# The planner of the first mixer and the second block charges a change between parts of TensorE's array, and runs one part in longer spells

## The chip, the cores and the metric

The kernel runs on one core of one Trainium2 chip, as one launch. The metric is the device time of the launch in microseconds (us), the median of three runs. Five engines work side by side, each in the order of its own program: PE (TensorE, matrix products; PEld is its weight loading), DVE (VectorE), ACT (ScalarE), POOL (GpSimd) and SP, which here only starts transfers. They wait for one another through semaphores.

## The reference, cut to what matters

All arrays are float32, one sequence of 256 tokens, width 1024. The first block is a modulated mixer (a state-space part, an attention part and a convolution part) followed by a mixture of 32 experts; the second block is an RWKV layer with 16 heads of 64, then a differential attention layer, each followed by a gated embedding. The part that this change moves most is the RWKV layer:

```python
    rkvg = jnp.einsum('cbsd,cde->cbse', xmix[:4], w_in)
    ...
    def step(state, inp):
        r_t, w_t, k_t, v_t, kk_t, a_t = inp
        s_kk = jnp.einsum('bhij,bhj->bhi', state, kk_t)
        state = (state * w_t[:, :, None, :]
                 - s_kk[..., None] * (kk_t * a_t)[:, :, None, :]
                 + v_t[..., None] * k_t[:, :, None, :])
        return state, jnp.einsum('bhij,bhj->bhi', state, r_t)
    ...
    _, y = lax.scan(step, state0, (seq_first(r), seq_first(decay), seq_first(k),
                                   seq_first(v), seq_first(kk), seq_first(a)))
    ...
    return y @ w_out
```

## The kernel before, in words

**Stages.** `mixer` does the first block up to the routing (until about 230 us in the profile), `moe` the experts (until about 688 us), `second` the rest. Within `second`, the RWKV layer runs until about 1051 us, then come its output projection, the eight pairs of attention heads (`diff_head`, about 1110 to 1230 us) and the last projection.

**The RWKV layer.** The recurrence is cut into four chunks of 64 tokens and done as products. Two of the 16 heads form one unit n, of eight. `dense` (a long list of matmuls written `pd<-xm,whl`, 768 of them, 256 columns each, 128 rows by 128 columns of the array) makes r, k, v and the gate: each product of two float32 numbers is three matmuls in type float32r of split parts. Each unit n then goes through three pieces of code, each a chain of small steps: `rwkv_inner` (scales, decays, the matrices BK, AR and PQ; matmuls into pm and pq), `rwkv_invert` (a triangular inverse in five levels: 8 matmuls `pi<-T,PQ` of 64 by 64, a copy by ACT, 8 matmuls `pi<-Gt,T`, a masked copy and a transpose by DVE, then the next level) and `rwkv_chunks` (four chunks in a row: `pe<-VU,PQ`, a copy by DVE, `pe<-W,Gt`, a copy by DVE, `pe<-VU,KB`, and so on). At most two units may be in the same piece. These small matmuls are float32 and use a part of the array: 64 by 64, 64 by 128, 128 by 64 or 32 by 32. The 768 dense matmuls use the whole. A float32 matmul shows as two records in the trace, a float32r one as one.

**What sets the order.** In `mixer` and `second` (not in `moe`) no order is written by hand. Every piece is a generator (a stream) that yields its next operations. `Plan` keeps, for each engine, the time at which it will be free by the planner's own costs (`cost`, L198), and for each tile the times of its last uses. `Mux.run` (L317) picks again and again: of all operations that head a stream it takes the engine of the one that can start first, adds that engine's hold to this time, and issues, of the operations of that engine that can start by then, the one of best rank. Ranks are small for the chains (0 to 2) and 3 for `dense`, so a small matmul that is ready goes ahead of a dense one. `start` (L194) gives the time at which an operation can start: when its inputs are ready and the engine free. `clocked` (L231) adds up how much work PE gets and doubles a matmul's cost when it was little; `cool` (L242) says that PE has had little work lately (below `HEAT`), and then `run` lets only float32r matmuls through, if one is ready. `enter` (L248) books the operation. What the streams issue is always the same set of instructions; the planner decides their order on each engine, and that order is fixed in the program. All recorded operations carry line 72.

Of the kernel before, what the change touches and what calls it, by code (L numbers as in the profile page):

```python
# [44 lines left out]
NR = _o  # L45


HEAT = 3500, 3550
HOLD = 250
WAIT = (60, 105, 110, 150), (60, 120, 120, 150)  # L50
FIRST = 3
# [85 lines left out]
class Plan:  # L137
# [8 lines left out]
    def __init__(s, nc):  # L146
        s.nc = nc
        s.at = {}
        s.use = {}
        s.free = {}  # L150
        s.work, s.past, s.part, s.heat = {}, [], False, HEAT[0]
        s.log = []
        s.cur = None
        for n in ("tensor", "vector", "scalar", "gpsimd", "sync"):
            setattr(s, n, Lane(s, getattr(nc, n), n))

    def reset(s):

        s.at = {"dma": 0.0, "scalar": 10e3, "gpsimd": 11e3, "tensor": 16e3, "vector": 15.8e3}
        s.use, s.free, s.work, s.past, s.heat = {}, {}, {}, [], HEAT[1]  # L160

    def __getattr__(s, x):
        return getattr(s.nc, x)
# [29 lines left out]

    def start(s, op, lag=0):  # L194
        eng = op.lane.name
        return op.ready if eng == "sync" else max(op.ready + lag * (eng == "tensor"), s.at.get(eng, 0.0))

    def cost(s, op):  # L198
        eng, name, out, ins = op.lane.name, op.op, op.outs[0], op.ins
        n = 1  # L200
        for _, c in (ins[-1] if name in ("tensor_reduce", "bn_stats") else out).ap[1:]:
            n *= c
        if eng == "tensor":
            if name == "transpose":
                return 109
            if ins[0].dtype == F32R:
                return max(107, n / 2.4) + 2
            m = out.ap[0][1]
            if m > 64:
                return max(214, n * 4 / 2.4 + 4)  # L210
            if s.box(out)[0]:
                return 22 if m <= 32 else 53
            return max(107, n * 4 / 2.4) + 2
        psum = any(x.space == PSUM for x in (out, *ins))
        if eng == "vector":
            fast = name in ("tensor_scalar", "tensor_copy", "memset") and not psum
            return 68 + n * (0.52 if fast else 1.04) + 61 * s.pointers(op)
        if eng == "scalar":
            return (51 if psum else 93) + n * 0.835 + 93 * s.pointers(op)
        if eng == "sync":  # L220
            return n * 512 / 355.0
        return 150 + n * 2.1

    @staticmethod
    def pointers(op):
# [2 lines left out]
            x += [op.a[i] if len(op.a) > i else None for i in ((2,) if op.op[0] == "s" else (2, 3))]  # L228
        return sum(isinstance(v, bass.AP) for v in x)

    def clocked(s, start, dur, op):  # L231

        w = int(start / 3413.3)
        n = 1 if op.ins[0].dtype == F32R else 2
        for _, c in op.outs[0].ap[1:]:
            n *= c
        n *= op.ins[0].ap[0][1] / 128 * (dur > 53)
        s.work[w] = s.work.get(w, 0.0) + n
        s.past.append((start, n))
        return dur if s.work.get(w - 1, 0.0) > 3060 else 2 * dur  # L240

    def cool(s, t):  # L242

        while s.past and s.past[0][0] < t - 3413.3:
            s.past.pop(0)
        return sum(n for _, n in s.past) < s.heat

    def enter(s, op, r):  # L248
# [6 lines left out]
        else:  # L255
            start = s.start(op)
            if eng == "tensor":

                part = op.outs[0].ap[0][1] <= 64
                dur = s.clocked(start, dur + 54 * (s.part and op.ins[0].dtype == F32R), op)  # L260
                s.part = part
            end = start + dur
            s.at[eng] = end
            if op.op == "dma_start":
# [19 lines left out]
class Mux:  # L284
# [32 lines left out]
    def run(s):  # L317
        pl = s.plan
        while s.st:
# [7 lines left out]
                            x.then()  # L327
            if not s.st:
                break
            can = [(pl.start(o, x.lag), x.rank if o.lane.name == "tensor" else x.side, i, x, o) for i, x in enumerate(s.st) for o in x.head]  # L330
            assert can, [(x.gen.__name__, x.gen.gi_frame.f_lineno) for x in s.st]
            t, _, _, x, o = min(can, key=lambda c: c[:3])
            eng = o.lane.name
# [2368 lines left out]
```

## Time and profile before

| what | value |
| --- | --- |
| median of 3 runs | 1298.44 us (1293.02 to 1301.1) |
| the profiled execution | 1295.23 us, of which the span from first to last instruction is 1293.3 us |
| busy over the span | PE 92%, PEld 63%, DVE 51%, ACT 34%, POOL 10% |
| mean granted TensorE clock | 0.948 of 2.4 GHz |

The page cuts the span into 40 slices; each digit is the busy share of an engine in tenths, and PEclk is the granted clock in tenths of full speed. TensorE has two clock levels, 2.4 GHz (1.00 in the rows) and 1.2 GHz (0.50); a value between them is a mean over a stretch. PE counts as busy from the start of a matmul to its modelled end, and matmuls overlap, so a PE that is always busy may still issue more or fewer of them in the same time. How fast it issues is read from the distance of two starts in the timeline.

### The profile page before, as it was taken

What the parts mean: (1) busy time and instruction counts of PE and PEld (TensorE: products, weight loads), DVE (VectorE), ACT (ScalarE), POOL (GpSimd) and SP (SyncE); (2) the same over time, 40 slices, a digit from 0 to 9 for tenths busy, and PEclk for the clock granted to TensorE, in tenths of its full rate; (3) what the DMA queues carried; (4) which work ended last, traced back from release to release, by engine and by line L of the source; (5) the groups of instructions that cost most, each with busy time, mean ns of one, the idle gap of its engine ahead of it and who ended that gap; (6) DMA issues with size and microseconds to landing.
All of it is one profiled execution on the core that took longest, in us unless ns stands there. A gap on an engine that the chain in (4) does not pass through costs nothing. (4 is left out here: it accounts for less than half of the span.)

```text
span 1293.3 us, 20461 instructions
## 1 busy us (share of the span) xinstructions
PE 1185.9 (92%) x7906; PEld 809.4 (63%) x7906; DVE 660.4 (51%) x1782; ACT 435.3 (34%) x1074; POOL 127.6 (10%) x358
## 2 busy tenths in 40 slices
PE   5999987999999989898986989999999989899896
PEld 3777886344343444444356867877777656888775
DVE  5695766111111111111027952576676677788885
ACT  3564543011110101111024721333344445655543
POOL 1000000000000000000000211222222002022212
PEclk8999996999999999999996975899999999899999
DMA  9658566899999999999983421111212342544422
GB/s 374 276 225 331 217 254 259 335 421 421 420 420 421 420 420 421 420 421 420 420 324 101 143 70 38 38 54 39 70 57 92 129 141 86 170 157 148 141 82 75
DMA packets 52628, 306.14 MB, mean 237 GB/s; under 512 B 5680, under 2 KB 10288, under 8 KB 25392
## 3 DMA queue, kind: packets, MB, share of 16 engines
q1 hardware_dynamic: 52368, 304.67, 60.1%
q8 instruction: 64, 1.05, 0.3%
q14 instruction: 36, 0.29, 0.1%
q0 software_dynamic: 160, 0.13, 0.1%
HBM read 302.55 MB, written 2.10 MB: 236 GB/s over the span
## 5 line engine op out<-in xcount | busy, mean ns | idle before, releaser
L366 PE MATMUL pgu<-w,xe 128*64 128x512 f32 x1024 | 233.0, 595 | 15.6 <-DMA w<-moe 15.6
L366 PEld LDWEIGHTS pgu<-w,xe 128*64 128x64 f32 x1024 | 80.9, 137 | 155.8 <-issue 116.6
L72 PE MATMUL pd<-xm,whl 128*128 128x256 f32 x768 | 149.3, 324 | 5.5 <-ACT xm L72 3.9
L72 DVE TENSOR_TENSOR whl<-raw,whl 128x512 fp32r<-128x512 f32 x192 | 128.4, 683 | 11.0 <-ACT whl L72 10.3
L72 ACT CAST whl<-raw 128x512 fp32r<-128x512 f32 x192 | 111.3, 618 | 40.5 <-PE pd L72 23.7
L72 PEld LDWEIGHTS pd<-xm,whl 128*128 128x128 f32 x768 | 112.9, 207 | 18.5 <-ACT xm L72 4.5
L366 PE MATMUL py<-w,hT 128*64 128x512 f32 (+1 forms) x528 | 116.6, 583 | 7.0 <-ACT hT L1408 7.0
L1433 DVE SCALAR_TENSOR_TENSOR yl<-py,ws,yh 128x512 fp32r<-128x512 f32 (+1 forms) x33 | 24.2, 734 | 123.4 <-ACT yh L1432 123.4
L366 PEld LDWEIGHTS py<-w,hT 128*64 128x64 f32 x528 | 40.7, 137 | 71.4 <-issue 54.7
L1352 POOL TENSOR_TENSOR PW<-P,wt 128x256 f32<-128x256 f32 x16 | 9.9, 617 | 617.7 <-PE pw L1413 213.4
L1432 ACT ACTIVATE yh<-py,ws 128x512 fp32r<-128x512 f32 (+1 forms) x33 | 22.2, 675 | 119.6 <-PE acc L366 66.1
L1398 DVE TENSOR_TENSOR hid<-hid,pgu 128x512 f32<-128x512 f32 x16 | 11.0, 688 | 98.2 <-PE pgu L366 98.1
L1397 DVE SCALAR_TENSOR_TENSOR hid<-hid,pgu 128x512 f32<-128x512 f32 x16 | 11.0, 688 | 96.8 <-ACT hid L1396 96.7
L72 PE MATMUL pd<-hh,whl 128*128 128x256 f32 x384 | 59.0, 295 | 1.4 <-ACT whl L72 0.8
L72 PE MATMUL pd<-xx,whl 128*128 128x256 f32 x384 | 54.2, 287 | 1.7 <-ACT whl L72 0.9
L72 PEld LDWEIGHTS pd<-hh,whl 128*128 128x128 f32 x384 | 50.6, 194 | 4.8 <-issue 2.6
L72 PE MATMUL pd<-whl,hh 128*128 128x512 f32 x192 | 52.4, 407 | 1.1 <-ACT hh L72 1.1
L72 PEld LDWEIGHTS pd<-xx,whl 128*128 128x128 f32 x384 | 48.9, 192 | 3.5 <-ACT whl L72 1.2
L72 PE MATMUL a<-hl,wh 128*128 128x256 f32 x160 | 47.1, 294 | 1.5 <-DVE hl L72 1.5
L72 PE MATMUL a<-hh,wh 128*128 128x256 f32 x160 | 46.8, 292 | 0.6 <-DVE x L72 0.6
L72 PE MATMUL a<-hh,wl 128*128 128x256 f32 x160 | 46.5, 291 | 0.0
L72 DVE TENSOR_TENSOR wl<-w,wh 128x512 fp32r<-128x512 f32 (+1 forms) x60 | 39.3, 692 | 10.5 <-ACT wh L72 10.4
(506 smaller groups left out, 2230.3 us busy)
## 6 DMA issues: line engine op xcount, KB each, us to landing
w<-moe SPq DMA_DIRECT2D x190, 1024.0 KB, 19.8
w<-ada SPq DMA_DIRECT2D x12, 2048.0 KB, 11.8
raw<-awin SPq DMA_DIRECT2D x32, 512.0 KB, 3.4
raw<-bwin SPq DMA_DIRECT2D x32, 512.0 KB, 3.5
w<-win SPq DMA_DIRECT2D x5, 2048.0 KB, 12.0
raw<-pleg SPq DMA_DIRECT2D x16, 512.0 KB, 3.3
w<-wout SPq DMA_DIRECT2D x2, 2048.0 KB, 8.6
raw<-awout SPq DMA_DIRECT2D x8, 512.0 KB, 3.4
```

Of the source, the lines that this page charges most:

```text
L72: r = s.fn(*s.a, **s.k)
L366: return s.nc.tensor.matmul(out, lhsT=lhsT, rhs=rhs, start=first, stop=last, **kw)
L1352: G.tensor_tensor(PW.rearrange(four, e=2), P[:, :, o:o + 128].bitcast(F32).rearrange(four, e=2), wt[:, :, 2 * i:2 * i + 2, None].to_broadc ...
L1397: V.scalar_tensor_tensor(hid, hid, 1.0, pgu[0], op0=OP.add, op1=OP.mult)
L1398: V.tensor_tensor(hid, hid, pgu[1], op=OP.mult)
L1432: A.activation(y[0], p, AF.Copy, scale=ws)
L1433: V.scalar_tensor_tensor(y[1], p, ws, y[0].bitcast(F32), op0=OP.mult, op1=OP.subtract)
```

## The change

The planner's model of PE is replaced; no operation is added or taken away. The part of the array that a matmul uses (`form`: rows and columns, each 128, 64 or 32) is now looked at. `start` adds 95 ns (138 when the clock is thought low) to the start of a matmul whose part differs from the one before it (`change`). `run` picks by a new time `come`: the same with that surcharge, but without it once PE has stayed long enough in its present kind of work (400 ns in float32, 1400 ns in float32r). The costs of small matmuls are set anew, a float32r one costs 9 ns more, the first float32r matmul behind another part 105 ns more, and the work by which the planner guesses the clock is weighted by part and kind. `HEAT` goes from 3500 and 3550 to 3300.

```diff
-HEAT = 3500, 3550
 ...
+WORK = {(128, 128): 3.2, (64, 64): 1.7, (64, 128): 2.2, (128, 64): 1.9, (32, 32): 1.5, (128, 32): 1.0}
+HEAT = 3300, 3300
+LONG = 400, 1400
 ...
     def start(s, op, lag=0):
         eng = op.lane.name
-        return op.ready if eng == "sync" else max(op.ready + lag * (eng == "tensor"), s.at.get(eng, 0.0))
+        if eng == "tensor":
+            return max(op.ready + lag, s.at.get(eng, 0.0) + s.change(op))
+        return op.ready if eng == "sync" else max(op.ready, s.at.get(eng, 0.0))
+
+    def come(s, op, lag=0):
+
+        t = s.start(op, lag)
+        if op.lane.name == "tensor":
+            at = s.at.get("tensor", 0.0)
+            if at - s.since > (LONG[s.whole]):
+                t = max(op.ready + lag, at)
+        return t
 ...
             if ins[0].dtype == F32R:
-                return max(107, n / 2.4) + 2
-            m = out.ap[0][1]
-            if m > 64:
-                return max(214, n * 4 / 2.4 + 4)
-            if s.box(out)[0]:
-                return 22 if m <= 32 else 53
-            return max(107, n * 4 / 2.4) + 2
+                return max(107, n / 2.4) + 11
+            k, m = s.form(op)
+            if k == m:
+                if k == 128:
+                    return max(214, n * 4 / 2.4 + 4)
+                return 58 if m == 64 else 31
+            if k == 64:
+                return max(107, n * 4 / 2.4) * (0.75 if n > 128 else 1) + 2
+            if m == 64:
+                return 58 if n < 8 else 165 if n <= 64 else 109
+            return 13 if s.box(out)[0] else max(107, n * 2 / 2.4) + 14
 ...
+    def form(op):
+
+        if op.op == "transpose":
+            return 128, 128
+        return tuple(128 if n > 64 else 64 if n > 32 else 32 for n in (op.ins[0].ap[0][1], op.outs[0].ap[0][1]))
 ...
+    def change(s, op):
+
+        op = getattr(op, "ops", [op])[0]
+        if s.part is None or s.part == s.form(op) or (s.part, s.form(op)) == ((64, 128), (128, 128)):
+            return 0
+        return 138 if s.cold(s.at.get("tensor", 0.0)) else 95
 ...
     def clocked(s, start, dur, op):
 ...
+        part, whole = s.form(op), op.ins[0].dtype == F32R
+        cold = s.cold(start)
+        if cold:
+            dur = 2 * (dur - 11) if whole else 1.9 * dur
+
+        if whole and part != s.part:
+            dur += 165 if cold else 105
+        n = 1.0 if whole else 1.5 if op.op == "transpose" else WORK[part]
 ...
-            can = [(pl.start(o, x.lag), x.rank if o.lane.name == "tensor" else x.side, i, x, o) for i, x in enumerate(s.st) for o in x.head]
+            can = [(pl.come(o, x.lag), x.rank if o.lane.name == "tensor" else x.side, i, x, o) for i, x in enumerate(s.st) for o in x.head]
```

**How the order moves.** Counted over PE's whole program of `second` (3244 matmuls in both), two neighbours use different parts of the array 540 times before and 331 times after; from matmul 200 to matmul 2000, the RWKV layer with its chains, 506 times and 299 times. In `mixer` it is 57 times in both, in `moe` 68 times in both.

The first place is on PE, in the inverse of the first unit, where `dense` (pd, the whole array) fills in between the 64 by 64 matmuls of a level (pi; `x8` stands for eight matmuls). A row is the source line, the operation, the tile written from the tiles read, and the size of the output. Before, in the trace at about 765 to 768 us:

```order
L72 MATMUL pi_5804<-T,PQ 64x64 x7
L72 MATMUL pq<-AR,BK 128x128
L72 MATMUL pd_5713<-xm_4945,whl 128x256 x3
L72 MATMUL pi_5804<-Gt,T 64x64 x5
L72 MATMUL pd_5713<-xm_4945,whl 128x256
L72 MATMUL pi_5804<-Gt,T 64x64
L72 MATMUL pd_5713<-xm_4945,whl 128x256
L72 MATMUL pi_5804<-Gt,T 64x64
L72 MATMUL pd_5713<-xm_4945,whl 128x256
L72 MATMUL pi_5804<-Gt,T 64x64
L72 MATMUL pd_5713<-xm_4945,whl 128x256
```

The same levels of the first unit's inverse in the changed program:

```order
L76 MATMUL pi_5817<-T,PQ 64x64 x8
L76 MATMUL pm<-ident,rkv 128x128 x2
L76 MATMUL pd_5748<-xm_4945,whl 128x256 x8
L76 MATMUL pm<-ident,BK 128x128 x4
L76 MATMUL pi_5817<-Gt,T 64x64 x8
L76 MATMUL pi_5858<-T,PQ 64x64 x8
L76 MATMUL pd_5748<-xm_4945,whl 128x256 x3
L76 MATMUL pm<-la,whl 128x256
```

The eight matmuls of a level, which stood in four pieces with single dense matmuls between them, now stand together, and so do the dense ones.

The second place is on PE in the middle of the layer, the third level of the fourth unit's inverse, beside the chunks of the third unit (pe). Before:

```order
L72 MATMUL pi_6947<-T,PQ 64x64 x3
L72 MATMUL pd_6889<-xm_4945,whl 128x256 x2
L72 MATMUL pe_6915<-VU,KB 128x128
L72 MATMUL pe_6915<-VU,PQ 64x64
L72 MATMUL pd_6889<-xm_4945,whl 128x256
L72 MATMUL pe_6915<-VU,PQ 64x64
L72 MATMUL pd_6889<-xm_4945,whl 128x256
L72 MATMUL pi_6947<-T,PQ 64x64
L72 MATMUL pd_6889<-xm_4945,whl 128x256 x2
L72 MATMUL pi_6947<-T,PQ 64x64 x3
```

The same level of the same unit in the changed program:

```order
L76 MATMUL pe_6968<-W,Gt 64x64 x2
L76 MATMUL pi_6979<-T,PQ 64x64 x8
L76 MATMUL pm<-ident,rsq_y 64x128
L76 MATMUL pe_6968<-VU,KB 128x128
L76 MATMUL pe_6968<-VU,PQ 64x64 x2
L76 MATMUL pi_6979<-Gt,T 64x64 x8
L76 MATMUL pm<-ident,rsq_y 64x128
L76 MATMUL pe_7024<-ST_4959,AR 128x128
L76 MATMUL pe_7024<-VU,PQ 64x64 x2
```

The dense matmuls are gone from between the pieces of the two chains; they stand further on, eleven in a row.

The third place is SP's list of the weight loads in the mixer (`win` for the dense products there, `ada` for the modulation). Before:

```order
L72 DMA w<-ada 128x4096 x3
L72 DMA w<-win 128x4096
L72 DMA w<-ada 128x4096
L72 DMA w<-win 128x4096
L72 DMA w<-ada 128x4096 x2
```

And in the changed program:

```order
L76 DMA w<-ada 128x4096 x2
L76 DMA w<-win 128x4096
L76 DMA w<-ada 128x4096 x3
L76 DMA w<-win 128x4096
L76 DMA w<-ada 128x4096
```

The first of these `win` loads stands one place earlier on the queue, the second behind one `ada` load more.

## Rows read from the trace of the kernel before

**Rows 1.** The page: span, busy time and share, busy tenths by slice, clock.
```profile
span 1293.3 us, 20461 instructions
PE 1185.9 (92%) x7906; PEld 809.4 (63%) x7906; DVE 660.4 (51%) x1782; ACT 435.3 (34%) x1074; POOL 127.6 (10%) x358
PE   5999987999999989898986989999999989899896
PEclk8999996999999999999996975899999999899999
```

**Rows 2.** Busy time by stage: the stretch, its length, busy us (instructions), clock, DMA.
```profile
core 0: us, PE busy (x) PEld busy (x) DVE busy (x) ACT busy (x) POOL busy (x), PEclk, DMA share, GB/s
60.00:160.00 100.00, 100.00 (x747) 80.24 (x745) 74.51 (x226) 57.30 (x147) 0.00 (x0) 1.00 0.66 263
...
240.00:660.00 420.00, 396.60 (x1990) 177.69 (x1987) 68.82 (x113) 46.48 (x74) 9.25 (x15) 1.00 1.01 420
...
688.00:740.00 52.00, 45.80 (x324) 43.05 (x325) 47.78 (x120) 30.34 (x76) 5.55 (x10) 0.87 0.44 141
740.00:756.00 16.00, 9.75 (x81) 7.82 (x80) 12.69 (x32) 4.80 (x12) 7.37 (x23) 0.90 0.41 133
756.00:771.00 15.00, 15.00 (x109) 11.63 (x110) 4.95 (x12) 3.66 (x10) 0.00 (x0) 0.73 0.15 45
771.00:821.00 50.00, 50.00 (x295) 37.24 (x294) 15.89 (x43) 9.67 (x26) 3.38 (x13) 0.50 0.11 35
821.00:1024.00 203.00, 198.77 (x2083) 155.40 (x2083) 141.84 (x417) 79.52 (x207) 51.21 (x192) 1.00 0.22 73
...
1120.00:1220.00 100.00, 92.25 (x740) 85.28 (x738) 86.43 (x206) 56.42 (x168) 23.21 (x78) 1.00 0.46 149
```

**Rows 3.** Waits of PE from 756 to 1024 us: total us, times, longest.
```profile
PE pe L72 <- DVE yn L72: 1.7, 2, 1.4
PE pi L72 <- DVE T L72: 0.9, 2, 0.5
```

**Rows 4.** Timeline of PE at full clock: start, length, operation, records.
```profile
766.04 0.33 PE L72 MATMUL pi<-Gt,T 64*64 64x64 f32 x2
766.30 0.38 PE L72 MATMUL pd<-xm,whl 128*128 128x256 f32 x1
766.61 0.33 PE L72 MATMUL pi<-Gt,T 64*64 64x64 f32 x2
```

**Rows 5.** Timeline of PE, the same pattern at half clock.
```profile
773.16 0.47 PE L72 MATMUL pi<-Gt,T 64*64 64x64 f32 x2
773.56 0.58 PE L72 MATMUL pd<-xm,whl 128*128 128x256 f32 x1
774.07 0.47 PE L72 MATMUL pi<-Gt,T 64*64 64x64 f32 x2
```

**Rows 6.** Timeline of PE, longer runs of one part at full clock.
```profile
714.01 12.10 PE L72 MATMUL pd<-xm,whl 128*128 128x256 f32 x98
...
827.93 1.09 PE L72 MATMUL pd<-xm,whl 128*128 128x256 f32 x7
828.95 0.45 PE L72 MATMUL pi<-Gt,T 64*64 64x64 f32 x8
829.33 0.49 PE L72 MATMUL pq<-AR,BK 64*128 64x128 f32 x2
...
864.03 0.68 PE L72 MATMUL pi<-Gt,T 64*64 64x64 f32 x16
864.64 0.44 PE L72 MATMUL pm<-ident,rkv 128*128 128x128 f32 x2
```

**Rows 7.** Waits of PE from 735 to 756 us.
```profile
PE pq L72 <- DVE BK L72: 3.6, 2, 3.0
PE pm L72 <- POOL rsq_y L72: 2.7, 1, 2.7
```

**Rows 8.** Waits of PE in the first 60 us.
```profile
PE x L72 <- DMA w<-ada: 4.2, 2, 3.5
```

**Rows 9.** DMA issues on the page: tile, queue, count, KB each, median us to landing.
```profile
w<-win SPq DMA_DIRECT2D x5, 2048.0 KB, 12.0
```

More of the change, by code (lines that the diff above doesn't have):

```diff
@@ L45 @@
 NR = _o
-HEAT = 3500, 3550
+SPELL = 3413.3
+WORK = {(128, 128): 3.2, (64, 64): 1.7, (64, 128): 2.2, (128, 64): 1.9, (32, 32): 1.5, (128, 32): 1.0}
+HEAT = 3300, 3300
+LONG = 400, 1400
 HOLD = 250
@@ L150, in __init__ @@
         s.free = {}
-        s.work, s.past, s.part, s.heat = {}, [], False, HEAT[0]
+        s.work, s.past, s.part, s.heat, s.whole, s.since = {}, [], None, HEAT[0], False, 0.0
         s.log = []
@@ L159, in reset @@
         s.at = {"dma": 0.0, "scalar": 10e3, "gpsimd": 11e3, "tensor": 16e3, "vector": 15.8e3}
-        s.use, s.free, s.work, s.past, s.heat = {}, {}, {}, [], HEAT[1]
+        s.use, s.free, s.work, s.past, s.part, s.heat, s.whole, s.since = {}, {}, {}, [], None, HEAT[1], False, 0.0
     def __getattr__(s, x):
@@ L229, in pointers, with cold @@
         return sum(isinstance(v, bass.AP) for v in x)
-    def clocked(s, start, dur, op):
-        w = int(start / 3413.3)
-        n = 1 if op.ins[0].dtype == F32R else 2
+    @staticmethod
+    def form(op):
+        if op.op == "transpose":
+            return 128, 128
+        return tuple(128 if n > 64 else 64 if n > 32 else 32 for n in (op.ins[0].ap[0][1], op.outs[0].ap[0][1]))
+    def cold(s, t):
+        return s.work.get(int(t / SPELL) - 1, 0.0) < 2880
+    def change(s, op):
[3 more added lines that the diff above has]
+        return 138 if s.cold(s.at.get("tensor", 0.0)) else 95
+    def clocked(s, start, dur, op):
+        part, whole = s.form(op), op.ins[0].dtype == F32R
[5 more added lines that the diff above has]
+        n = 1.0 if whole else 1.5 if op.op == "transpose" else WORK[part]
         for _, c in op.outs[0].ap[1:]:
             n *= c
-        n *= op.ins[0].ap[0][1] / 128 * (dur > 53)
-        s.work[w] = s.work.get(w, 0.0) + n
+        w, end = int(start / SPELL), start + dur
+        behind = max(0.0, min(1.0, (end - (w + 1) * SPELL) / dur))
+        s.work[w] = s.work.get(w, 0.0) + n * (1 - behind)
+        s.work[w + 1] = s.work.get(w + 1, 0.0) + n * behind
         s.past.append((start, n))
-        return dur if s.work.get(w - 1, 0.0) > 3060 else 2 * dur
+        if whole != s.whole:
+            s.whole, s.since = whole, start
+        s.part = part
+        return dur
     def cool(s, t):
-        while s.past and s.past[0][0] < t - 3413.3:
+        while s.past and s.past[0][0] < t - SPELL:
             s.past.pop(0)
@@ L257, in enter @@
             if eng == "tensor":
-                part = op.outs[0].ap[0][1] <= 64
-                dur = s.clocked(start, dur + 54 * (s.part and op.ins[0].dtype == F32R), op)
-                s.part = part
+                dur = s.clocked(start, dur, op)
             end = start + dur
```

## The prediction

> **What bounds the kernel now.** I read the page first, then the busy time by stage, then PE's waits and its timeline in the one stage that the change reorders much. The page says that PE is busy for 92% of the span and that its clock has a hole in the slices around 60% of the span [rows 1]. By stage [rows 2], the experts (240 to 660 us) are bound by transfers: 420 GB/s at a DMA share of 1.01, and the planner doesn't order that stage. In the mixer PE is busy in all of 60 to 160 us. From 688 to 740 us DVE is busy for 47.78 of 52 us: it prepares the mixed inputs of the RWKV layer, and PE waits for it. From 756 to 1024 us, the body of the RWKV layer, it is the other way round: PE is busy for 15.00 of 15, 50.00 of 50 and 198.77 of 203 us, DVE for 70% of the last stretch, and PE's waits in the 268 us are a few us [rows 3]. So whatever PE issues faster there comes off the end, until DVE or the chains of small steps are late.
>
> Two things make PE slow in that body. The first is the change between parts of the array. At full clock one dense matmul and one 64 by 64 matmul (two records) that alternate take 766.61 - 766.04 = 0.57 us a pair [rows 4]. In a long run a dense matmul takes 12.10 / 98 = 0.123 us; a run of 16 records of 64 by 64 takes 864.64 - 864.03 = 0.61 us, one of 2 records 766.30 - 766.04 = 0.26 us, so a record costs (0.61 - 0.26) / 14 = 0.025 us [rows 4, 6]. The pair's own work is 0.123 + 0.05 = 0.17 us; the other 0.40 us goes to its two changes, 0.20 us each. A second reading gives a little less: seven dense matmuls and a run of 8 records take 829.33 - 827.93 = 1.40 us, of which 0.86 + 0.20 us is work, which leaves 0.34 us for two changes, 0.17 us each [rows 6]. The second thing is the clock: 0.50 in all of 771 to 821 us, 0.73 in the 15 us ahead of it, 1.00 from 821 us on [rows 2]. Ahead of the fall to 0.50 PE did such pairs [rows 4], and it was still in them 2 us after [rows 5]. There a pair takes 774.07 - 773.16 = 0.91 us [rows 5], 1.6 times as long, so a us at the low clock does 0.63 us of work and loses 0.37 us.
>
> **The change part by part.** Nothing is added or removed; the order of `second` and of `mixer` moves.
>
> *Fewer changes of part.* 540 - 331 = 209 fewer in `second`, nearly all in the RWKV layer (506 to 299), where PE is the bound. At 0.17 to 0.20 us they are worth 36 to 42 us at full clock; I take 40, near the upper price, because most of the removed ones lie between dense and small matmuls, as in the first place shown.
>
> *The clock.* The 50 us at the low clock lose 50 x 0.37 = 19 us. What stood ahead of the fall, pairs with one dense matmul each, is replaced there by runs of eight dense ones and of eight or sixteen small ones, so PE does more work in the same time; I take the 19 us in full, with 0 as the other bound. The earlier dip, in the 0.73 of 756 to 771 us, I leave as it is: it follows PE's waits for DVE and POOL at 740 to 756 us (9.75 of 16 us busy [rows 2, 7]), which the change doesn't remove.
>
> The Trainium skill, "TensorE: Matmul & The Clock Gate", the section on what is happening, puts it so that the throttle is the state of an idle engine and that activity releases it. The rows don't bear that out as it stands: PE has no idle time in those 50 us and yet has the low clock. By that rule alone the fall would come of the waits before it, nothing in the order would lift it, and the 19 us would stay; that is the second case below.
>
> *What is late next.* Without these 59 us the body takes 268 - 59 = 209 us, and DVE still needs 4.95 + 15.89 + 141.84 = 162.7 us in it [rows 2]: 78% of the time instead of 61%. How much PE then waits I read from two stretches: at DVE 70% (821 to 1024 us) PE was idle for 2%, at DVE 86% (1120 to 1220 us) for 7.75% [rows 2]. On the line between them 78% gives 5%, 10 us of 209, against 4 us now: 6 us more. A chain's small matmul that is ready now also waits behind longer dense runs: eleven, as in the second place shown, are 11 x 0.123 = 1.4 us. Most of that is hidden, because three pieces of code for several units are under way; I add 3 us for what isn't. In sum 9 us, between 2 (as now) and 25 (12% of 209, PE's idle share at DVE 92% from 688 to 740 us [rows 2]).
>
> *The rest.* In `mixer` PE changes parts 57 times in both programs, so there is no gain by that. Its weight loads change places on SP's queue: a `win` load moved behind one more `ada` load, whose buffer comes free only when PE has used it, is late by up to one landing, 12.0 us [rows 9], if it were wanted at once; the other is earlier, and PE's 4.2 us of waiting for weights could shrink [rows 8]. PE is busy without a break from 60 to 160 us, which covers a late load of this size; I take 0, between -4 and +6 (half a landing). `moe` keeps its order. Outside the RWKV layer `second` has 32 changes instead of 34: 0.
>
> Sum: -40 - 19 + 9 + 0 = -50 us, against the profiled execution's own time (1295.23 us, span 1293.3 us): 1245 us. The median of the runs shown lies 3 us above that execution, which is less than the bounds here.
>
> **The rivals.** (a) The clock falls as before. For it: the waits at 740 to 756 us stay, so the body starts at the low clock again, and it took until 821 us to leave it. Against it: it was left in between, in the stretch from 756 to 771 us, with the longer runs still to come. Then only -40 + 9 = -31: 1264 us.
>
> (b) The chains become the bound, and the gain stays on PE. For it: a level of the inverse goes PE, ACT, PE, DVE, DVE, and there are five levels in a row; in the new order only a few small matmuls stand between the two halves of a level (second place shown), so PE stands still where a copy is late. Against it: with pieces of code so close together PE waited just a few us in 268 [rows 3]. To end within 1% of before it must give back 46 us or more of the 59, an idle share of 55 in 264 us, about 21%, nearly three times that of the stretch with DVE at 86%. Time: about 1291 us. Half as bad, 1270 us.
>
> (c) Slower: the low clock spreads. Runs of sixteen small matmuls follow each other without dense ones between; if PE drops to the low clock in these and stays there, each us of work takes 0.6 us more. The body is then 209 us of work at full clock; the gain of 50 is lost when 50 / 0.6 = 83 us of it run at the low clock, and it is slower by 1% from 83 + 13 / 0.6 = 105 us on. At three quarters of the body, 157 us, the time is 1245 + 94 = 1339 us. Against it: from 821 to 1024 us the clock held at 1.00 with an order that did less in the same time.
>
> (d) The change doesn't do what it says: excluded by the order, where the pieces do stand together.
>
> **How the numbers follow.** About 1% is what a measurement of this kernel can tell from no change (13 us). The forecast, -50 with terms between -36 and -42, up to -19, and +2 to +25, covers 1232 to 1260 us, and I give it 0.58. The clock as before (1264 us): 0.14. Chains half as bad (1270 us and up to 1285 us): 0.10. Chains eating nearly all (about 1291 us): 0.10. Slower by the clock: 0.06. Still faster than 1232 us, when waits stay as they are and the first dip goes too: 0.02. The range leaves out no more than 0.2 with 1228 to 1276 us. Faster by over 1% holds the first three and the last, 0.84; within 1% 0.10; slower 0.06.
>
> **What the changed profile would show.** Right: the timeline of the RWKV layer has hardly any single dense matmul between small ones; the clock is 1.00 in what corresponds to 771 to 821 us; the body from the first inverse to the last chunk is some 210 to 225 us, DVE is busy for about 75 to 80% of it, and PE's idle share is about 5%. The first term is wrong if a change in the new timeline costs much less than 0.17 us or lies beside a wait; the second if the clock has a hole as long as before; the third if PE's idle time there is above 25 us, with ACT or DVE named as the releaser of pi or pe. The mixer's end (about 230 us) and the experts' length should stay within 6 us. If PE's busy time falls by 50 us and the span doesn't, (b) holds.

## The result

| kernel | time, median (lowest to highest) | ratio to before, 95% interval |
| --- | --- | --- |
| before | 1298.02 us (1293.02 to 1301.1) | 1 |
| changed | 1252.15 us (1247.42 to 1257.9, one execution apart) | 0.9652 (0.9601 to 0.9703) |
| changed, timed again beside the experiments | 1254.8 us (1251.09 to 1255.84) | 0.9603 (0.9557 to 0.9648) |

The change saves 46 us; 50 were forecast. The execution set apart took 1824.46 us, with TensorE at 1.2 GHz nearly throughout (mean granted clock 0.555); all rows of the changed kernel below are of another one (1254.69 us, span 1252.9 us).

The page of the changed kernel: span, busy time and share, PE's busy tenths and clock over 40 slices, as in [rows 1].

```profile
span 1252.9 us, 20462 instructions
PE 1142.4 (91%) x7906; PEld 790.2 (63%) x7906; DVE 657.0 (52%) x1782; ACT 434.7 (35%) x1074; POOL 124.9 (10%) x358
PE   5999997899999999998987889999999988898896
PEclk9899998899999999999997787999999988999999
```

The same number of matmuls is executed, and PE is busy for 43.5 us less. By stage, as in [rows 2]: stretch, length, busy us of each engine (instructions), clock, DMA share, GB/s.

```profile
60.00:160.00 100.00, 100.00 (x727) 79.10 (x726) 72.68 (x223) 54.68 (x144) 0.00 (x0) 1.00 0.69 266
240.00:660.00 420.00, 396.62 (x1990) 177.17 (x1988) 68.83 (x113) 46.47 (x74) 9.25 (x15) 1.00 1.01 420
...
740.00:756.00 16.00, 12.53 (x84) 10.43 (x82) 10.41 (x24) 5.62 (x13) 7.56 (x24) 0.79 0.45 149
756.00:771.00 15.00, 14.07 (x117) 11.70 (x117) 7.95 (x23) 4.44 (x12) 0.00 (x0) 0.54 0.20 63
771.00:792.00 21.00, 20.94 (x334) 18.13 (x333) 17.05 (x50) 9.37 (x26) 5.17 (x17) 1.00 0.15 51
792.00:979.00 187.00, 182.59 (x2111) 152.02 (x2109) 140.36 (x422) 80.93 (x209) 47.20 (x188) 0.99 0.25 82
...
1064.00:1188.00 124.00, 110.65 (x848) 102.03 (x847) 97.02 (x226) 63.46 (x184) 25.28 (x78) 0.96 0.43 138
```

Mixer and experts are as before. The 50 us of 771 to 821 us at clock 0.50, with 295 records, are gone: about the same part of the program is now 21 us at 1.00, with 334 records. The last row is a loss: the attention heads take longer than before.

Since nothing but the order of the instructions differs, the two traces can be laid on each other by the number of a matmul in PE's program of `second` (0 to 3243). The table is worked out from the start of matmul k in both traces. "Low clock" is the time at 0.50 and "idle" the time without a running matmul; both in us.

| matmuls of `second` | before | changed | difference | changes of part | low clock | idle |
| --- | --- | --- | --- | --- | --- | --- |
| 200 to 400: first inverse starts | 38.8 | 41.2 | +2.4 | 28, now 21 | 10.2, now 20.3 | 6.3, now 5.2 |
| 400 to 600: where the hole was | 53.2 | 21.2 | -32.0 | 82, now 27 | 50.2, now 0.2 | 0.0, now 0.1 |
| 600 to 2000: rest of the RWKV layer | 231.1 | 207.9 | -23.2 | 396, now 251 | 1.0, now 3.4 | 5.7, now 5.5 |
| 2000 to 2200: gated embedding, start of attention | 59.3 | 64.4 | +5.1 | 0 | 10.2, now 13.7 | 6.9, now 10.8 |
| 2200 to 3000: attention heads | 113.5 | 124.1 | +10.6 | 28, now 28 | 0.0, now 10.2 | 8.4, now 13.3 |
| 3000 to the last | 59.3 | 54.9 | -4.4 | 6, now 4 | 0.0, now 0.0 | 5.3, now 1.9 |

The RWKV layer (200 to 2000) gains 52.8 us, what stands behind it loses 11.3. With 1 us more ahead of matmul 200 that is the 40.4 us between the two spans; the medians, over several executions, differ by 46. (The profiled execution of before was one of its quicker ones: span 1293.3 us, against a median of 1297.3 us in 27 executions timed beside the experiments.)

### The profile page after: what moved, and what is told of

The parts are those of the page before. It is cut to its first block, busy times and chain, and to the rows that moved or that the text cites. A ratio compares the mean times of both kernels' runs of the same rounds, so it can differ in the third digit from the quotient of the medians.

```text
span 1822.7 us, 20462 instructions
## 1 busy us (share of the span) xinstructions
PE 1759.6 (97%) x7906; PEld 1077.9 (59%) x7906; DVE 664.5 (36%) x1782; ACT 437.7 (24%) x1074; POOL 119.3 (7%) x358
## 5 line engine op out<-in xcount | busy, mean ns | idle before, releaser
L411 PE MATMUL pgu<-w,xe 128*64 128x512 f32 x1024 | 395.9, 964 | 0.0
L411 PE MATMUL py<-w,hT 128*64 128x512 f32 (+1 forms) x528 | 199.0, 939 | 4.3 <-ACT hT L1453 4.3
L76 PE MATMUL pd<-xm,whl 128*128 128x256 f32 x768 | 173.9, 388 | 5.2 <-ACT xm L76 3.9
L76 PEld LDWEIGHTS pd<-xm,whl 128*128 128x128 f32 x768 | 154.9, 292 | 12.2 <-ACT xm L76 4.5
L76 PE MATMUL pd<-xx,whl 128*128 128x256 f32 x384 | 87.3, 390 | 1.1 <-ACT whl L76 1.1
L76 PE MATMUL pd<-hh,whl 128*128 128x256 f32 x384 | 87.5, 392 | 0.8 <-DVE whl L76 0.7
L76 PE MATMUL pd<-whl,hh 128*128 128x512 f32 x192 | 81.1, 586 | 2.1 <-ACT hh L76 2.1
L76 PEld LDWEIGHTS pd<-hh,whl 128*128 128x128 f32 x384 | 77.6, 276 | 5.7 <-issue 2.4
L76 PEld LDWEIGHTS pd<-xx,whl 128*128 128x128 f32 x384 | 77.9, 280 | 3.6 <-ACT whl L76 1.3
L411 PEld LDWEIGHTS acc<-pt,yh 128*128 128x128 f32 x128 | 34.7, 271 | 46.0 <-issue 46.0
```

Of the source, the lines that this page charges most:

```text
L76: r = s.fn(*s.a, **s.k)
L411: return s.nc.tensor.matmul(out, lhsT=lhsT, rhs=rhs, start=first, stop=last, **kw)
```

## The experiments

All kernels of this section but three (the changed kernel itself, the one without the rule for spells and the one with doubled spells throughout) carry the old planner and the new one side by side; a switch by stage and by the number of matmuls already issued in `second` says which one rules. With the switch wholly on one side the order is that of before or of the changed kernel. In the diffs `NEW = (mixer, second)` is that switch. Each ratio is to the kernel before as it was timed again beside that kernel, with medians of 1301.67, 1296.1 and 1302.77 us on the three occasions; so a difference of a few us between kernels of different occasions is read from the stretches of their traces, not from medians or ratios.

**Which stage.** The changed kernel, timed again beside the others:

> The changed kernel once more, for a profile at an undisturbed clock. By the prediction's own steps (theory I: fewer changes of part, and the clock hole filled) the time is about 1250 us, the clock in the RWKV layer's body is 1.00 from the first inverses on, PE's idle time in the body is about 10 us and the body takes 210 to 225 us. Theory II (the clock falls as before): a hole of about 50 us at 0.50 stays in the trace, and then the gain must come of changes worth more than 0.2 us each. Theory III (the mixer gives the gain): the RWKV layer's body is as long as before and the mixer ends some 40 us sooner.

Measured: 1254.8 us, ratio 0.9603.

Only `second` has the new planner:

```diff
+NEW = (lambda n: False, lambda n: True)
```

> The new planner in the second block alone, the old one in the mixer (the second block's order is that of the changed kernel, the mixer's that of the kernel before). Theory I: 1250 us, within 5 us of the changed kernel. Theory III: 1280 to 1295 us.

Measured: 1253.8 us (1251.65 to 1257.55), 0.9601 (0.9554 to 0.9649). Only the mixer has it:

```diff
+NEW = (lambda n: True, lambda n: False)
```

> The new planner in the mixer alone, the old one in the second block. Theory I: 1298 us, no difference that can be measured (between -4 and +6 us by the prediction). Theory III: 1255 to 1275 us.

Measured: 1307.17 us (1293.58 to 1319.54), 1.0017 (0.9968 to 1.0065), no change (the kernel before took 1294.37 to 1313.52 us beside it). All of the gain is made in `second`, and the moved weight loads of the mixer cost nothing that can be seen.

**The front of the RWKV layer against the rest.** The new planner rules the first 600 matmuls of `second` alone:

```diff
+NEW = (lambda n: False, lambda n: n < 600)
```

> The new planner for the first 600 matmuls of the second block alone (the first two units' inverses, where the clock was low before), the old one in the mixer and from matmul 600 on. It has 69 changes of part fewer than the kernel before (471 against 540). Theory I: 69 x 0.19 = 13 us for the changes and 19 us for the clock, so about 1268 us, and the stretch of about 50 us at the low clock is gone. Theory II (the low clock comes of the waits ahead of it and stays): only 13 us, 1285 us, with the low clock in the trace as before.

Measured: 1265.54 us, 0.9695 (0.9652 to 0.9738). Busy time of this kernel by stretch:

```profile
756.00:771.00 15.00, 15.00 (x160) 12.93 (x156) 7.54 (x21) 6.30 (x18) 0.00 (x0) 0.65 0.17 54
771.00:792.00 21.00, 20.95 (x321) 17.57 (x320) 15.36 (x45) 8.00 (x24) 5.17 (x17) 1.00 0.16 52
```

The counterpart: new for matmuls 600 to 2009, old ahead of them and behind.

```diff
+NEW = (lambda n: False, lambda n: 600 <= n < 2010)
```

> The new planner from matmul 600 to matmul 2010 of the second block alone: the first two units keep the old order with its single dense matmuls and the low clock. 148 changes of part fewer than before (392 against 540), none of them in the stretch where the clock was low. By the prediction's first step (0.17 to 0.20 us a change) it gains 25 to 30 us, less some 5 us of more waiting: 1274 to 1280 us, and the clock hole of 50 us stays. If the changes were worth only what the timeline of the alternating pairs shows at the low clock, or lay beside waits, the gain is below 15 us: over 1286 us.

Measured: 1277.64 us (1268.29 to 1279.89), 0.9819 (0.9759 to 0.9879). Its busy time by stretch:

```profile
769.00:824.00 55.00, 55.00 (x327) 41.78 (x328) 16.30 (x44) 10.38 (x28) 3.37 (x13) 0.50 0.10 32
824.00:900.00 76.00, 72.26 (x865) 61.14 (x866) 57.72 (x178) 31.34 (x86) 27.13 (x102) 0.96 0.17 56
```

The two halves come apart cleanly. With the new order in the first 600 matmuls the hole is gone (matmuls 400 to 600 in 21.2 us); with the old order there it stays (53.5 us), whatever comes later. All traces agree, that of the 1824 us set apart: in the three with the old order there, matmuls 400 to 600 have 41.0 to 51.0 us at the low clock, in the ten with a new one at most 4.4 us. PE has next to no idle time in either: 15.00 of 15 and 20.95 of 21 us busy in the one, 55.00 of 55 us in the other. In the one the clock rises, in the other it falls, and up to there the two kernels differ in the order alone: the order decides. The rest of the layer, matmuls 600 to 2000, takes 209.4 us in the new order with 248 changes of part, 231.1 in the old one with 396: 21.7 us for 148 changes, 0.15 us each. It holds 9.4 us more at the low clock (3.5 us at 0.37 each) and 1.4 us more of idle time; with these set apart a change is worth 26.6 / 148 = 0.18 us.

**The new planner without its rule.** The surcharge is taken out of the picking time; costs and clock model stay new:

```diff
-            if at - s.since > (LONG[s.whole]):
+            if at - s.since > -1:
```

> The changed kernel with the one rule for longer spells taken out: when the planner picks, a change of part is never charged (come always takes the time without the surcharge); the new costs, the surcharge in the booked times and the new clock model stay. It has 423 changes of part in the second block, between 331 (changed) and 540 (before). By the price of 0.19 us a change (theory I) the time is 92 x 0.19 = 17 us above the changed kernel, 1271 us, if the clock holds. If the better clock model alone makes the gain (theory II turned round), the time stays at 1253 us.

Measured: 1276.55 us, 0.9836 (0.9789 to 0.9882); 423 changes of part in `second`. The theory that the better clock model alone makes the gain (1253 us) fails. What stays of the new planner (the costs, the surcharge in the booked times, the clock model) gives some two fifths of the gain: with 47 changes in matmuls 400 to 600 the hole is nearly gone (25.6 us, 2.5 of it at the low clock). From 600 to 2000 it needs 231.6 us, as before, with 312 changes instead of 396. By the price per change it should be about 15 us quicker; 23.9 us at the low clock, against 1.0, and 3.0 us more of idle time take back about 11 of them (8.5 and 3.0); 4 stay unexplained. Over all of 200 to 2000 the same working comes out: 22.7 us for 119 changes, 13.7 us less at the low clock and 3.6 us more idle, which is 0.18 us a change. Whether the clock falls more often in this order than in that of before isn't shown by one execution of each: the old order of `second` has 1.0 us at the low clock between 600 and 2000 in the trace of before and 47.8 us in that of the kernel with the new planner in the mixer alone.

**Longer spells still.** A PE that stays twice as long in one kind of work:

```diff
-LONG = 400, 1400
+LONG = 800, 2800
```

> The changed kernel with the spells twice as long (800 and 2800 ns for 400 and 1400 ns). 324 changes of part against 331, so nearly nothing is left to gain on that side: -1 us. The prediction's third step says that small matmuls that are ready wait behind longer dense runs: if that costs what the step supposed, the time rises by 2 to 6 us, to about 1256 us; if chains were the bound (rival b), by 10 us or more.

Measured: 1278.15 us (1274.36 to 1282.44), 0.9853 (0.9799 to 0.9908), 23 us slower than the changed kernel with 324 changes instead of 331. The time near that of the changed kernel, which I had expected, was missed by over 20 us. Up to matmul 1600 its layer runs like that of the changed kernel (matmuls 200 to 1600 in 202.1 and 201.3 us, with 15.6 and 8.6 us of idle time and 17.1 and 23.9 us at the low clock); from 1600 to 2000 it takes 95.0 us against 69.0. Its busy time there, and then that of the changed kernel:

```profile
922.00:1018.00 96.00, 87.49 (x706) 62.14 (x704) 52.77 (x164) 34.43 (x82) 9.68 (x49) 0.80 0.27 91
```

```profile
930.40:999.40 69.00, 66.83 (x645) 49.29 (x644) 49.82 (x144) 33.91 (x81) 7.54 (x22) 1.00 0.46 150
```

The order shows a candidate: with longer spells `dense` is used up early, at matmul 1508 instead of 1745, and the last units' chains then run with little beside them. Groups of PE in this stretch, two of the kernel with doubled spells (922 to 1018 us) and then two of the changed one (930 to 999 us; operation, tiles, shape, count, busy us, mean ns, idle before and its releaser):

```profile
L76 PE MATMUL pe<-VU,PQ 128*64 128x64 f32 (+1 forms) x98 | 13.1, 267 | 0.7 <-DVE VU L76 0.7
L76 PE MATMUL pi<-T,PQ 64*64 64x64 f32 (+1 forms) x176 | 8.9, 245 | 2.2 <-DVE rsq_t L76 1.2 <-DVE T L76 1.0
```

```profile
L76 PE MATMUL pd<-xm,whl 128*128 128x256 f32 x48 | 7.7, 297 | 0.0
L76 PE MATMUL pi<-T,PQ 64*64 64x64 f32 (+1 forms) x144 | 6.2, 217 | 0.1
```

The changed kernel still has 48 dense matmuls there, the other none, and its small ones take longer (245 against 217 ns). Two kernels separate this from the other reading, that the chains lose by waiting behind long dense runs anywhere. One has the doubled spells up to matmul 1000 of `second` and those of the change behind it, so that dense matmuls last until number 1733:

```diff
-            if at - s.since > (LONG[s.whole]):
+            if at - s.since > (LONG[s.whole] if s.stage and s.count >= 1000 else LONG[s.whole] * 2):
```

> The kernel with doubled spells (800 and 2800 ns), but from matmul 1000 of `second` on with the spells of the change again; the dense matmuls then last until matmul 1733 (1745 in the changed kernel, 1508 with doubled spells throughout). Theory S: doubled spells cost nothing while there are dense matmuls to fill in with, and the 25 us were lost behind the last of them: 1255 - 5 (mixer) = 1250 us, at most 1256, and matmul 1600 to 2000 in about 69 us. Rival T: the longer waits of the chains cost time themselves, throughout the layer: then about half of the loss stays, 1262 to 1268 us.

Measured: 1255.5 us (1254.39 to 1259.15), 0.9669 (0.9615 to 0.9724). The other has them from matmul 1000 on only; its last dense matmul is number 1598:

```diff
-            if at - s.since > (LONG[s.whole]):
+            if at - s.since > (LONG[s.whole] * 2 if s.stage and s.count >= 1000 else LONG[s.whole]):
```

> The changed kernel with doubled spells from matmul 1000 of `second` on only; the dense matmuls are used up at matmul 1598. Theory S (no filler left is what costs): 1255 + 15 to 25 = 1270 to 1280 us, the loss behind matmul 1600 and PE waiting there for DVE and ACT, with clock dips. Rival T (longer waits of the chains): about half of the loss, 1265 us, spread from matmul 1000 on.

Measured: 1278.45 us (1276.22 to 1281.26), 0.9844 (0.9788 to 0.9899). Busy time of the first one and of the second one over matmuls 1600 to 2000:

```profile
928.90:1000.50 71.60, 67.90 (x654) 48.91 (x653) 50.45 (x147) 34.43 (x83) 8.12 (x24) 1.00 0.45 145
```

```profile
924.90:1014.10 89.20, 80.31 (x690) 57.97 (x690) 52.57 (x162) 35.56 (x86) 13.62 (x53) 0.81 0.30 98
```

The loss belongs to the missing filler: where it lasts, the stretch takes 71.6 us at clock 1.00, where it is used up, 89.2 us at 0.81. More than half of either loss is the clock: 34.1 us at 0.50 cost 12.6 of the 20 us here, 37.6 us cost 13.9 of the 26 with doubled spells throughout, and 6 to 7 us are idle time. Longer spells by themselves cost little: matmuls 200 to 1600 take 205.2 us in the first one, 4 us more than in the changed kernel, with 5.7 us more of idle time in 600 to 2000.

**The loss in the attention heads.** New planner for the RWKV layer only, old one in the mixer and behind matmul 2010:

```diff
+NEW = (lambda n: False, lambda n: n < 2010)
```

> The new planner for the first 2010 matmuls of the second block (the RWKV layer) alone, the old one in the mixer and in all that comes behind (the attention heads, both projections). In the changed kernel the RWKV layer came out 53 us shorter, but what follows it 11 us longer (from matmul 2000 to the end 243.9 us against 232.5 us). Theory P: the new planner's own order costs these 11 us in the attention heads, where PE's transposes of a head's output (pi from on) now stand earlier in its program and wait for POOL (10.7 us against 6.8 us). Then this kernel takes 1242 us, about 11 us less than the changed kernel. Theory Q: the heads are slower because the layer before them ends sooner and weights or DVE are behind; then the 11 us stay and the time is 1253 us.

Measured: 1246.27 us (1244.97 to 1248.17), 0.9604 (0.9557 to 0.9651). Matmuls 2200 to 3000 take 113.4 us in it, as before, where the changed kernel takes 124.1. Theory P holds for the heads but not for all of the 11 us: matmuls 2000 to 2200 still take 63.4 us, and the gain from 2000 on is 8 us. (The ratio is that of the changed kernel, 0.9604 against 0.9603, since the kernel before ran faster beside this one; the times of the launch don't show the gain, the stretch in the traces does.) PE's largest wait in the heads, before, in the changed kernel and in this one:

```profile
PE pi L72 <- DVE on L72: 6.8, 6, 1.3
```

```profile
PE pi L76 <- DVE on L76: 10.7, 6, 2.1
```

```profile
PE pi L78 <- DVE on L78: 6.8, 6, 1.3
```

These are the transposes `pi<-ident,on` of a pair of heads' output, whose input is scaled by a root from POOL. In PE's program the first one is matmul 2412 of the changed kernel and 2425 of the one before: it stands 13 matmuls earlier, and PE waits longer for its input. To see which part of the planner moves it, only the table of costs goes back behind matmul 2010:

```diff
+NEWKINDS = ('start', 'come', 'cool', 'clocked')
...
+    def new(s, kind):
+        return s.stage == 0 or s.count < 2010 or kind in NEWKINDS
...
+            if not s.new("cost"):
+                if ins[0].dtype == F32R:
+                    return max(107, n / 2.4) + 2
...
```

> The changed kernel, in which only the table of matmul costs goes back to the old one behind matmul 2010 of `second` (output projection, attention heads, last projection); the surcharge for a change of part, the clock model and the order up to there stay new. Theory Q: the 8 us by which the changed kernel loses against the kernel with the old planner behind the RWKV layer (1254.8 against 1246.3 us) come from the new costs: dense matmuls count for more, so the planner thinks PE later than it is and puts the transposes of a head's output (pi<-ident,on, first one at matmul 2412 instead of 2425) ahead of dense ones while their input is not ready. With the old costs they stand at 2422, 2536, 2648: then 1246 us (1242 to 1249), matmul 2200 to 3000 in 113 to 116 us, and PE's waits for `on` about 7 us as before. Rival R: the surcharge or the clock model does it: 1255 us, 124 us for that stretch, waits for `on` above 10 us.

Measured: 1244.78 us (1241.71 to 1246.33), 0.9573 (0.9533 to 0.9612). The heads in this kernel: busy time, and PE's wait.

```profile
1061.50:1176.00 114.50, 105.37 (x850) 97.89 (x849) 96.32 (x224) 62.00 (x182) 21.39 (x78) 1.00 0.47 152
```

```profile
PE pi L78 <- DVE on L78: 5.6, 6, 1.3
```

The stretch is back at 114.5 us, the clock at 1.00 and the wait at 5.6 us, while surcharge and clock model (with its 105 ns for the first float32r matmul behind another part, where the old planner added 54) are still the new ones. So it is the new costs. In the stretch of the changed kernel idle time accounts for 4.9 us of the 10.6 and the low clock, 10.2 us of it at 0.37 us each, for 3.8; 1.9 us stay open. Behind the heads 4.4 us come back (the last row of the table), so that heads and last projection lose 6.2 us together.

**A combination.** Old planner behind the RWKV layer, new one in the RWKV layer, and doubled spells in the mixer:

```diff
+NEWKINDS = ()
...
+        return s.stage == 0 or s.count < 2010 or kind in NEWKINDS
...
-            if at - s.since > (LONG[s.whole]):
+            if at - s.since > (LONG[s.whole] if s.stage else LONG[s.whole] * 2):
```

> A combination: new planner in the mixer with twice the longer spells (800 and 2800 ns), new planner with the spells of the change in the RWKV layer, old planner behind it. The kernel with doubled spells throughout had its mixer end 5 us sooner than all others. Theory M: that was the order of the mixer, so 1246 - 5 = 1241 us (1238 to 1245), and the span's first 230 us end 5 us sooner again. Rival N: it was chance of that execution: 1246 us (1243 to 1250).

Measured: 1245.02 us (1241.99 to 1250.54), 0.9582 (0.9538 to 0.9627), as without the doubled spells. The mixer's first product of the routing (px) starts at 218.2 us here. In the two others with doubled spells in the mixer it starts at 215.5 (doubled throughout) and 218.5 us (doubled up to matmul 1000). In three executions with the changed kernel's order of the mixer it starts at 216.8 (late doubled spells), 220.3 (old costs in the heads) and 221.9 us (the changed kernel): most of the 5 us is within what one and the same order scatters. The clock goes with it: in these three the first 240 us hold 23.9, 27.3 and 34.1 us at the low clock.

The three kernels that leave the costs or the whole planner old behind the RWKV layer lie at 1244.8 to 1246.3 us, the three measurements of kernels with all of `second` under the new one at 1252.15 to 1254.8. These are medians of different occasions, and the intervals of the ratios overlap; that they are faster rests on the stretch of 113.4 to 114.5 us in their traces against 122.4 and 124.1 us in the two of the others.

## Why the prediction came out right

**The bound.** PE was the bound of the RWKV layer and still is. From 771 to 979 us it is busy for 203.53 of 208 us, and what it issues faster came off the end. Matmuls 351 to 1898, which are the 268 us of the prediction, take 212.1 us: inside the 210 to 225 expected. (They end with the last inverse; the chunks of the last unit follow for another 21 us before and 27 us now, which the prediction's words on where the layer ends passed over.)

**Step 1, the changes of part: -40 forecast, -38 found.** Of the 52.8 us, the low clock takes 61.4 - 23.9 = 37.5 us less, at 0.37 us each 13.9 us, and idle time fell by 1.2 us. The rest, 37.7 us, is for 506 - 299 = 207 changes: 0.18 us each, inside the 0.17 to 0.20 read from pairs and runs in [rows 4, 6]. The kernel with the new order from matmul 600 on bears it out by itself, with 22 us for 148 changes. The timeline of the changed kernel where the hole was (start, length, operation, records):

```profile
773.51 0.74 PE L76 MATMUL pm<-la,whl 128*128 128x256 f32 x4
774.09 0.99 PE L76 MATMUL pd<-xm,whl 128*128 128x256 f32 x7
775.01 0.68 PE L76 MATMUL pi<-Gt,T 64*64 64x64 f32 x16
775.53 0.63 PE L76 MATMUL pi<-T,PQ 64*64 64x64 f32 x16
776.09 0.40 PE L76 MATMUL pm<-tab,BK 128*64 128x2 f32 x8
776.42 1.57 PE L76 MATMUL pd<-xm,whl 128*128 128x256 f32 x11
```

The pairs of [rows 4] are gone; 7 and 11 dense matmuls stand together, and a level of 16 records is issued in half a microsecond.

One thing no kernel here separates: nearly all of the changes that went are changes of the number type too, from a dense float32r matmul to a small float32 one or back. Between matmuls 200 and 2000 the neighbours that differ in part and type fall from 323 to 114; those that differ in part alone go from 183 to 185, in type alone from 68 to 91. (`LONG` counts its spells by type as well.) The trace of the changed kernel tells them apart, at clock 1.00. A transposition (`ident`) is a float32 matmul on the whole array, and shows as one record. Between dense matmuls only the type changes:

```profile
828.54 0.60 PE L76 MATMUL pd<-xm,whl 128*128 128x256 f32 x3
828.98 0.28 PE L76 MATMUL pe<-ident,yn 128*128 128x128 f32 x1
829.02 1.68 PE L76 MATMUL pd<-xm,whl 128*128 128x256 f32 x12
```

Between small float32 matmuls only the part changes:

```profile
815.80 0.33 PE L76 MATMUL pi<-Gt,T 64*64 64x64 f32 x4
816.06 0.33 PE L76 MATMUL pe<-ident,yn 128*128 128x128 f32 x1
816.32 0.33 PE L76 MATMUL pi<-Gt,T 64*64 64x64 f32 x2
816.60 0.47 PE L76 MATMUL pe<-ST,AR 128*128 128x128 f32 x2
```

In the first rows three dense matmuls and the transposition take 829.02 - 828.54 = 0.48 us. The dense ones need 3 x 0.123 = 0.37 us, which leaves 0.11 us for the transposition with both changes of type, no more than transpositions in a run take from start to start (0.11 us). In the second rows three small matmuls and a transposition take 816.60 - 815.80 = 0.80 us, of which 0.15 + 0.11 us is work: 0.18 us for each of three changes of part. Over thirteen traces, at 1.00 and without idle time, a change of type alone costs 0.01 us (221 places) and a change of part alone, between 64 by 64 and 64 by 128 or 128 by 64, 0.16 to 0.20 us (112 places). So it is the part. Not every change costs as much: between dense and 64 by 128 matmuls it is 0.09 us (86 places).

The 0.37 us for a us at the low clock, which the prediction read from one pair and which this working uses throughout, has a second reading: over 27 executions of the kernel before, whose time at the low clock (worked out from the granted clock) lies between 124 and 184 us, the span grows by 0.37 us with each us of it.

**Step 2, the clock: -19 forecast, -14 found.** The hole went in full, as said: 50.2 us at the low clock became 0.2, worth 18.5 us. The first dip stayed, as said, and grew: from 10.2 to 20.3 us (0.79 and 0.54 in 740 to 771 us of the stages above), which takes 3.7 us back; 2.4 us more at the low clock from matmul 600 on take another 0.9. (Another execution of the same order has 13.7 us in it, so the size scatters.) The waits ahead of it are those of [rows 7] in part (POOL `rsq_y`, 2.7 us again). The case that the clock falls as before is excluded by the pair of kernels above, in which the hole goes and stays with the order of the first 600 matmuls. The Trainium skill, "TensorE: Matmul & The Clock Gate", the section on what is happening, says that activity releases the throttle. If activity is busy time, the trace doesn't agree: in the kernel that keeps the hole PE is busy in 55.00 of 55 us at 0.50. What activity would have to mean instead, no run here shows.

**Step 3, what is late next: +9 forecast, -1 found.** This term was too big. DVE's share from 771 to 979 us is 157.42 / 208 = 76%, near the 78% foreseen, but PE's idle share is 4.47 / 208 = 2%, not 5%: as in the stretch of DVE at 70% in [rows 2]. The line through two stages misled, since the heads' 7.75% came of one chain, the wait for `on`, and not of DVE's share. PE's waits from 756 to 1012 us, the largest ones:

```profile
PE pd L76 <- ACT hh L76: 2.3, 1, 2.3
PE pe L76 <- DVE yn L76: 2.0, 4, 0.8
PE pq L76 <- DVE BK L76: 1.4, 1, 1.4
```

They are of the size of [rows 3]; the first stands behind the recurrence. The 3 us for waits behind longer dense runs were not found either. The rival in which the chains become the bound fails here, but the runs showed from where it is true: when `dense` is used up before the last units' chains, it costs 20 to 26 us, clock dips included.

**Step 4, the rest: 0 forecast, +11 found.** For the mixer it holds: its planner alone changes nothing (1.0017), and the weights' loads land no later (9.3 us instead of the 12.0 of [rows 9]). For `second` behind the RWKV layer it fails. "Outside the RWKV layer `second` has 32 changes instead of 34: 0" counted the one thing that the change is named for. But the edit also sets new costs for every matmul, and these decide where a small matmul is put among hundreds of dense ones. A transpose that the planner believes ready 13 matmuls sooner holds PE, with all that is queued behind it; three dips of the clock stand in that stretch. The diff showed the costs, and the order of the heads was there to be compared; the prediction went by the order of the RWKV layer alone.

The heads and the last projection are 6.2 us of this loss. The rest is the 5.1 us from matmul 2000 to 2200. It appears in every kernel with the new order up to the end of the layer, whichever planner rules behind it (63.4 us with the old one, 64.6 with the old costs). There PE waits for the last chunk's output with nothing left to do:

```profile
1006.58 1.66 PE L76 MATMUL pd<-whl,hh 128*128 128x512 f32 x6 [2.28 <-ACT hh L76]
1008.08 0.85 PE L76 MATMUL pq<-whl,hh 128*128 128x512 f32 x3
1008.77 0.85 PE L76 MATMUL pi<-whl,hh 128*128 128x512 f32 x3
1012.41 0.77 PE L76 MATMUL pm<-ident,hT 128*128 128x128 f32 x4 [2.79 <-DVE hT L76]
```

Before, these two waits are 1.15 and 1.07 us, and four `pi<-ple` products stand between them; now those products have all been issued ahead of the first one. That the moved products cause the longer waits is read from the two traces and was not tried by itself.

**The sum.** -38 - 14 - 1 + 11 = -42 against -50, and 1 us was lost ahead of matmul 200: two misses of about 10 us in opposite directions, one in the step on the stage that I had studied and one in the stage that I had not, and a clock term 5 us short. That the two misses nearly cancel is luck; the two large terms, on which the forecast stood, are not. (The range of 1232 to 1260 us is too narrow above for the prediction's own terms: -36 - 19 + 25 + 6 = -24 gives 1271 us. The result lies inside either.) Between the profiled executions the difference is 40, between the medians 46 us.

## What to carry to other kernels

Where PE has no idle time, count the changes between parts of the array in its program and price one from a pair and a run in the trace; here 207 fewer at 0.18 us were worth most of the gain, and the new order of the first 600 matmuls took away the stretch at the low clock as well. Where the neighbours differ in more than the part, find places in the trace where only one thing changes. Filler work is a stock: rules that spend it faster early leave the last dependent chains bare, so look at where its last instruction stands. When a planner's costs are edited, compare the order in all stages that it plans, above all where a single transposition waits for a long chain; a cost that is right for one stage can put such an instruction too early in another.

## What was not expected of the hardware

- An engine that is never idle can stay at 1.2 GHz for 50 us, and 55.00 of 55 us in the kernel that keeps the old front; another order of the same instructions, with as little idle time, was at 2.4 GHz by 771 us. What decides it inside the order is open. One execution of an order doesn't tell its time at the low clock: between matmuls 600 and 2000 the order of before had 1.0 us in one execution and 47.8 in another, the changed order 3.4 and 13.7.
- The price of a change of part is the same over a whole layer (0.18 us, the low clock set apart) as in the pairs and runs of [rows 4, 6], although the layer's runs of one part are now 1800 / 299 = 6.0 matmuls long instead of 1800 / 506 = 3.6: it doesn't hide behind a longer run. Read place by place between dense and 64 by 64 matmuls, at 1.00 and without idle time in thirteen traces, it is 0.20 us where both stand singly (39 places) and 0.20 us where both runs hold seven or more (61 places).
- One order of the mixer ends 5 us apart from execution to execution (216.8 to 221.9 us), with 23.9 and 34.1 us at the low clock; that is nearly as much as the 6.2 us which heads and last projection lose by the planner's costs.
